# Seven-product projections of six key heads and of the key latents, through memory, ahead of the attention

## The chip, the cores and the metric

The kernel runs on one core of one Trainium2 chip. The metric is the device time of one execution in microseconds. The engines are TensorE (PE; its weight loads are PEld), VectorE (DVE), ScalarE (ACT), GpSimd (POOL) and SyncE (SP); the last issues most of the DMAs, and POOL issues some.

## What is computed

One layer of a streaming encoder with two groups of attention heads that share one input projection, followed by an output projection and a gated feed-forward part. Rows: 512 frames of a new stream with 16 meta tokens ahead, and 64 frames of a running stream with 128 cached rows: T = 592 rows, 2048 wide, all in 32-bit floats.

```python
h = rmsnorm(x, norm_attn_g)
z = h @ w_in          # columns: Q of 8 heads | K of 8 | V of 8 | query latents 512 | key latents 256 | rotary key 64
# group A, 8 differential heads (two 64-wide halves c share one V of 128):
s = einsum('bqhcd,bkhcd->bhcqk', qd, kd) * DIFF_SCALE + bias
p = softmax(where(visible, s, neg));  p = p[:, :, 0] - lam * p[:, :, 1]
o_d = rmsnorm(p @ vd, diff_subln_g) * (1 - lam_init)
# group B, 8 heads over normalised latents with a rotary key:
o_m = latent_attention(...)
x = x + concat(o_d, o_m) @ w_out
x = x + (silu(h2 @ w_gate) * (h2 @ w_up)) @ w_down      # h2 = rmsnorm(x, norm_ffn_g)
```

New keys, values and latents are outputs too.

## The kernel before, in words

Every 32-bit product is made of three fast ones: weights and data are split into a high and a low part (ACT writes the high part at L156, `wh`; DVE subtracts it for the low part at L153, `wl`), and `wh*xh`, `wh*xl`, `wl*xh` are added up in one PSUM bank. A projection of 128 columns (`project`, L225) takes 16 blocks of 128 input rows x 3 products x 2 halves of the tokens, 96 matmuls of 296 columns (288 where only the queries' 576 rows are wanted). Its weights come in two loads of 512 KB (`wr`, two buffers, on SP's queue).

Stages:

1. To 47 us: x is transposed block by block (`transpose_x`), scaled by the norm's gain, split into `xh` and `xl`, which stay on chip; the unscaled block is stored to `xspill` (L484). Beside it head 0's Q and K are projected into `ps0` and `ps1` (`project_both`). The norm's factor of each row is not applied yet: `rb`, a tile with it, scales each projection's result.
2. 47 to about 495 us: the eight differential heads. `diff_attend` (L639) makes the scores in pieces of up to 400 columns (tile `sp`, two banks; L108 on TensorE, with q and its low part), DVE adds the bias and takes the row's extreme (L665), ACT takes the exponential (L669), DVE weights the two halves (L673 to L677, tiles `ls`, `e`, `p`). Products with V follow, then the norm of the result, whose factor DVE works out in three steps of 576 columns (`rsqrt_apart`, L178, L180, L182). While a head is attended, the projections of later heads (`projections`, L725: Q, K and V of each head, in this order) fill TensorE between the pieces. A projection's result is scaled by DVE into a tile `z` (queries L732, keys L739, values L790), turned by `twin_queries`, `keys` and `values` into operands (`q00h` and so on, `kk`, `vh`, `vl`), and transposed for the outputs (tiles `pna`, `pnb`; `natural`, L568). `pck` is the transposed cached key.
3. 495 to 745 us: the latent heads, with the output projection as fill. `second_part` projects query latents (four column blocks), key latents (blocks 4 and 5) and the rotary key.
4. To the end: the rest of the output projection, then the feed-forward part, which already multiplies by seven products (`winograd`, L1262). Its sums of weights (L1300, POOL and DVE) and of tokens (`difference`, L1230 on POOL, split at L1218 on ACT and L1219 on DVE, after ACT's scaling at L1363) are the nearest relatives of the new stage's rows.

What sets the order: for stages 2 and 3 the class `Streams` (L39) advances the generators; each names the time until it goes on (`yield 3.0`), or a list of generators that it waits for (`yield [att[h - 2]]`: until head h - 2's attention is done), or takes a PSUM bank (`take("ps")`), and among the ready ones the lowest rank goes. `projections` has rank 25, below all attention work. TensorE's instructions keep the order in which they are issued; the other engines' are ordered by a scheduler. Each engine runs its own list in order, so a row that waits holds up all behind it. `skew` (L339) copies a bias row into a skewed form in memory on POOL's queue; `diff_attend` loads it on SP's queue (tile `bias`) and clears a corner of it with a memset on POOL (L642).

Of the kernel before, what the change touches and what calls it, by code (L numbers as in the profile page):

```python
# [19 lines left out]
P = 128  # L20
# [78 lines left out]
class OrderedTensorEngine:  # L99
# [5 lines left out]
    def matmul(self, out, lhsT, rhs, start, stop):  # L105
        n = int(np.prod(rhs.shape[1:]))
        self.streams.now += max(n, 256) * (0.00042 if rhs.dtype == F32R else 0.00168)
        self.tc.keep_in_program_order(self.pe.matmul(out, lhsT, rhs, start=start, stop=stop))  # L108
# [7 lines left out]
def encoder_step(  # L116
# [213 lines left out]
    xspill = dp.tile([KC, P, TQ], F32, name="xspill")  # L330
# [15 lines left out]
    with ExitStack() as ph:  # L346
# [42 lines left out]
        with tc.tile_pool(name="xn", bufs=1, reuse_waits="tile") as xn:  # L389
# [83 lines left out]
            def transpose_x(kc):  # L473
# [11 lines left out]
                store(xspill[kc], xt[:, 0:TQ])  # L485
# [64 lines left out]
        pss.close()  # L550
        pst = ph.enter_context(tc.tile_pool(name="pst", bufs=1, space=PSUM, reuse_waits="tile"))
        pso = ph.enter_context(tc.tile_pool(name="pso", bufs=1, space=PSUM, reuse_waits="tile"))
        psv = pss.enter_context(tc.tile_pool(name="psv", bufs=1, space=PSUM, reuse_waits="tile"))
# [171 lines left out]
        def projections():  # L725
# [3 lines left out]

            def queries(h, ps):  # L730
                z = ztile()
                V.scalar_tensor_tensor(hv(z, TQ), ev(ps, QH), DH ** -0.5, hv(rb, TQ),  # L732
                                       op0=ALU.mult, op1=ALU.mult)
                st.give("ps", 2.0)
                twinned[h] = st.spawn(0, twin_queries(qs[h % 2], z))

            def new_keys(h, ps):
                z = ztile()
                V.tensor_tensor(hv(z), ev(ps), hv(rb), op=ALU.mult)  # L739
                st.give("ps", 2.0)  # L740
# [3 lines left out]
            def row_factors():  # L744
                yield 4.0
                for name in ("tp", "po"):
                    yield from st.take(name)
                main, own = tbank("rm"), obank("ro")
                for j, (o, n) in enumerate(tok):
                    PE.matmul(main[:, o:o + n] if o < SEQ else own[:, 0:n], rc[0:n, j:j + 1].to_broadcast([n, P]),  # L750
                              ident[0:n, 0:n], start=True, stop=True)
                V.tensor_copy(rb[:, 0:SEQ], main)
                V.tensor_copy(rb[:, SEQ:T], own[:, 0:OWN])
                for name in ("tp", "po"):
                    st.give(name, 2.0)

            def first_rows():
                yield from row_factors()
                queries(0, ps0)
                yield 3.0  # L760
# [1014 lines left out]
```

## Time and profile before

| | us |
|---|---|
| median of 3 runs | 2362.17 (2360.29 to 2363.19) |
| profiled execution | 2363.54 |
| its span, first to last instruction | 2361.8 |
| TensorE busy in the span | 2331.1 (99%) |
| VectorE busy | 1862.5 (79%) |
| ScalarE busy | 1131.1 (48%) |
| GpSimd busy | 676.8 (29%) |

How to read it: the page gives busy times and shares over the span. A group's row names the line, the engine, the operation, output <- inputs, the shape, how many there were, and after the bar the busy time and the mean of one in ns, then the idle time ahead of them and what ended it. A timeline row begins with the start and the duration in us; in brackets stands the idle time ahead of it and what ended that. A row marked x2 stands for two instructions. A row of the windows begins with the stretch and its length, and then gives the busy time of PE, PEld, DVE, ACT and POOL with the number of instructions, the granted TensorE clock as a share of full speed, the DMA's share and GB/s. A row of the DMA issues gives the KB of one and the median us from issue to landing. Line numbers are those of the kernel before unless the text says otherwise.

### The profile page before, as it was taken

What the parts mean: (1) busy time and instruction counts of PE and PEld (TensorE: products, weight loads), DVE (VectorE), ACT (ScalarE), POOL (GpSimd) and SP (SyncE); (2) the same over time, 40 slices, a digit from 0 to 9 for tenths busy, and PEclk for the clock granted to TensorE, in tenths of its full rate; (3) what the DMA queues carried; (4) which work ended last, traced back from release to release, by engine and by line L of the source; (5) the groups of instructions that cost most, each with busy time, mean ns of one, the idle gap of its engine ahead of it and who ended that gap; (6) DMA issues with size and microseconds to landing.
All of it is one profiled execution on the core that took longest, in us unless ns stands there. A gap on an engine that the chain in (4) does not pass through costs nothing. (4 is left out here: it accounts for less than half of the span.)

```text
span 2361.8 us, 43545 instructions
## 1 busy us (share of the span) xinstructions
PE 2331.1 (99%) x17336; PEld 2299.9 (97%) x17336; DVE 1862.5 (79%) x2777; ACT 1131.1 (48%) x2005; POOL 676.8 (29%) x419
## 2 busy tenths in 40 slices
PE   9999999999999999999999999999999999999998
PEld 8999999999999999999999999999999999999997
DVE  6667776676666789888898888888888888888884
ACT  6455555444454554444454454454454333333435
POOL 0000000120001446555555555554555111111110
PEclk9999999999999999999999999999999999999999
DMA  8433343263334643444444544544546884654532
GB/s 257 118 93 93 102 118 86 73 188 96 114 93 156 186 151 102 158 154 136 158 149 136 163 142 138 168 133 147 167 132 201 312 289 137 230 181 156 181 90 99
DMA packets 361626, 353.10 MB, mean 150 GB/s; under 512 B 23751, under 2 KB 318446, under 8 KB 361422
## 3 DMA queue, kind: packets, MB, share of 16 engines
q1 hardware_dynamic: 359150, 345.78, 46.4%
q0 software_dynamic: 992, 3.48, 0.5%
q8 instruction: 136, 2.23, 0.4%
q10 hardware_dynamic: 1280, 1.06, 0.2%
q14 instruction: 68, 0.56, 0.1%
HBM read 268.82 MB, written 82.34 MB: 149 GB/s over the span
## 5 line engine op out<-in xcount | busy, mean ns | idle before, releaser
L1315 PE MATMUL m<-b,wh 128*128 128x288 f32 x7280 | 1062.9, 295 | 7.8 <-ACT wh L156 3.3
L1315 PEld LDWEIGHTS m<-b,wh 128*128 128x128 f32 x7280 | 994.6, 188 | 13.0 <-ACT wh L156 9.2
L1319 PE MATMUL m<-b,wl 128*128 128x288 f32 x3640 | 581.1, 296 | 2.3 <-DVE wl L153 2.0
L1319 PEld LDWEIGHTS m<-b,wl 128*128 128x128 f32 x3640 | 515.7, 189 | 4.7 <-DVE wl L153 4.5
L153 DVE TENSOR_TENSOR wl<-raw,wh 128x1024 fp32r<-128x1024 f32 (+2 forms) x347 | 477.3, 1377 | 38.9 <-ACT wh L156 38.4
L156 ACT ACTIVATE wh<-raw 128x1024 fp32r<-128x1024 f32 (+2 forms) x347 | 313.6, 904 | 363.7 <-PE m L1315 320.2
L1300 POOL TENSOR_TENSOR ws<-raw 128x1024 f32<-128x1024 f32 (+2 forms) x85 | 173.0, 2036 | 662.4 <-DVE wl L153 339.8
L156 ACT ACTIVATE wh<-ws 128x512 fp32r<-128x512 f32 (+2 forms) x248 | 196.7, 793 | 286.5 <-PE m L1315 126.0
L153 DVE TENSOR_TENSOR wl<-ws,wh 128x512 fp32r<-128x512 f32 (+2 forms) x248 | 240.3, 969 | 7.7 <-PE m L1319 4.3
L108 PE MATMUL ps<-xh,wh 128*128 128x296 f32 (+1 forms) x992 | 222.8, 306 | 0.3 <-ACT xh L160 0.3
L108 PE MATMUL ps<-xl,wh 128*128 128x296 f32 (+1 forms) x992 | 215.2, 298 | 0.4 <-DVE xl L161 0.3
L108 PE MATMUL ps<-xh,wl 128*128 128x296 f32 (+1 forms) x960 | 207.8, 298 | 0.0
L1574 DVE TENSOR_TENSOR y<-y,m 128x288 f32<-128x288 f32 x280 | 126.2, 451 | 65.3 <-PE m L1319 64.2
L1466 DVE TENSOR_TENSOR c<-c,s 128x288 fp32r<-128x288 f32 x172 | 170.3, 990 | 0.0
L108 PEld LDWEIGHTS ps<-xh,wh 128*128 128x128 f32 x992 | 159.9, 190 | 3.3 <-issue 1.1
L108 PEld LDWEIGHTS ps<-xl,wh 128*128 128x128 f32 x992 | 160.6, 189 | 1.1 <-DVE xl L161 0.9
L108 PEld LDWEIGHTS ps<-xh,wl 128*128 128x128 f32 x960 | 155.5, 189 | 0.0
L153 DVE TENSOR_TENSOR wl<-wr,wh 128x1024 fp32r<-128x1024 f32 (+1 forms) x109 | 117.3, 1077 | 42.6 <-ACT wh L156 38.9
L1300 POOL TENSOR_TENSOR raw<-raw 128x1024 f32<-128x1024 f32 (+1 forms) x46 | 141.0, 3064 | 3.5
L156 ACT ACTIVATE wh<-wr 128x1024 fp32r<-128x1024 f32 (+1 forms) x111 | 102.0, 918 | 81.4 <-PE ps L108 57.8
L1412 DVE TENSOR_TENSOR c<-c,m 128x288 f32<-128x288 f32 x171 | 73.1, 447 | 79.1 <-PE m L1319 41.1
L1485 POOL TENSOR_TENSOR c<-c,rb 128x576 f32<-128x576 f32 x44 | 74.9, 1702 | 138.0 <-ACT c L1484 138.0
(400 smaller groups left out, 3031.9 us busy)
## 6 DMA issues: line engine op xcount, KB each, us to landing
raw<-in_ffn_w_gate SPq DMA_DIRECT2D x44, 1024.0 KB, 6.1
raw<-in_ffn_w_up SPq DMA_DIRECT2D x44, 1024.0 KB, 7.9
b<-opspill SPq DMA_DIRECT2D x147, 288.0 KB, 6.0
raw<-in_ffn_w_down SPq DMA_DIRECT2D x32, 1024.0 KB, 5.9
wr<-in_w_in SPq DMA_DIRECT2D x57, 512.0 KB, 4.1
opspill<-s SPq DMA_DIRECT2D x43, 576.0 KB, 3.1
opspill<-c SPq DMA_DIRECT2D x43, 576.0 KB, 6.7
raw<-in_ffn_w_down SPq DMA_DIRECT2D x8, 1280.0 KB, 6.1
```

The lines of the kernel that those rows point to most:

```text
L108: self.tc.keep_in_program_order(self.pe.matmul(out, lhsT, rhs, start=start, stop=stop))
L153: V.tensor_tensor(lo, src, f32(hi), op=ALU.subtract)
L156: S.activation(hi, src, AF.Copy)
L1300: (G if p == 5 or p == 7 and within else V).tensor_tensor(x, y, z, op=ALU.add if p == 5 else ALU.subtract)
L1315: PE.matmul(banks[p], wh[:, k, :], x, start=first and new and k == 0 and x is hi, stop=False, skip_group_check=not new)
L1319: PE.matmul(banks[p], wl[:, k, :], hi, start=False, stop=last and k == n - 1, skip_group_check=not new)
L1412: V.tensor_tensor(c, c, banks[p], op=ALU.add)
L1466: V.tensor_tensor(src[:, k].bitcast(F32R), src[:, k], f32(hi[:, k]), op=ALU.subtract))
L1485: G.tensor_tensor(g[:, f, :], g[:, f, :], rb2, op=ALU.mult)
L1574: V.tensor_tensor(c, c, banks[p], op=ALU.add)
```

## The change

`xspill` keeps all 592 rows of x, and a new tile in memory, `zspill`, holds eleven projection results. Between stage 1 and the attention stands a new stage:

- V0 is projected first; within it `rb` is made and the results of Q0 (kept on chip as `z_first`) and K0 (to `zspill`) are scaled. Then Q1. Both results go to `zspill` (V0: 7, Q1: 8).
- Beside them the generator `token_sums` builds operands: for each of eight pairs of row blocks it loads the two blocks back from `xspill`, ACT scales them by the gain, POOL makes four differences of token halves in a chain (t = b12 - b11, t = b22 - t, t7 = b22 - b12, t = b21 - t; t is overwritten), and each is split into a high and a low part that stay on chip (32 tiles `s4` to `s7`).
- `seven` is called four times: key heads 1 and 2, 3 and 4, 5 and 6, and the two key latents. A call takes two blocks of 128 columns as the halves of a 2x2 block product (row blocks in even and odd positions, tokens in two halves): four weight loads of 512 KB (`quarter`; two into new tiles `wa`, two into the two buffers `wr`), four sums of weights (one on POOL, three on DVE), and seven products of 24 matmuls of 296 columns in the order 1, 2, 5, 6, 3, 7, 4, added up in PSUM or by DVE and ACT. The two results are scaled by `rb` and stored to `zspill`.

The attention then takes K0 to K6, V0, Q1 and the latents 4 and 5 from `zspill` by DMAs on POOL's queue (`spilled_rows`, L859 of the changed kernel), and `projections` makes only Q of heads 2 to 7, K of head 7 and V of heads 1 to 7.

```diff
-    xspill = dp.tile([KC, P, TQ], F32, name="xspill")
+    xspill = dp.tile([KC, P, T], F32, name="xspill")
+    zspill = dp.tile([11, P, T], F32, name="zspill")
...
+            def token_sums():
+                for m in range(KC // 2):
+                    rows_ = [sa.tile([P, T], F32, name="xr", tag=f"xr{t}", bufs=2) for t in range(2)]
+                    for t, r in enumerate(rows_):
+                        load(r, xspill[2 * m + t])
+                        S.activation(r, r, AF.Copy, scale=gA[:, 2 * m + t:2 * m + t + 1])
+                    (b11, b12), (b21, b22) = (halves(r) for r in rows_)
+                    yield
+                    def operand7(p, src):
+                        hl = sa.tile([P, 2, TH], F32R, name=f"s{p}_{m}")
+                        split(hl[:, 0], hl[:, 1], src)
+                        operands7[m, p] = hl[:, 0], hl[:, 1]
+                    t = sa.tile([P, TH], F32, name="ts", tag="ts", bufs=2)
+                    t7 = sa.tile([P, TH], F32, name="t7", tag="t7")
+                    G.tensor_tensor(t, b12, b11, op=ALU.subtract)
+                    operand7(5, t)
+                    G.tensor_tensor(t, b22, t, op=ALU.subtract)
+                    operand7(6, t)
+                    yield
+                    G.tensor_tensor(t7, b22, b12, op=ALU.subtract)
+                    operand7(7, t7)
+                    G.tensor_tensor(t, b21, t, op=ALU.subtract)
+                    operand7(4, t)
+                    yield
...
+            for n, _ in enumerate(project(pv0, w_in[:, OFF_V:OFF_V + P], xs1, ready=(both[4], both[5]))):
+                if n == 3:
+                    spread_factors()
+                    z_first = scaled_rows(ps0, None, QUERY_SCALE)
+                    scaled_rows(ps1, 0)
+                if n % 2:
+                    next(building)
+            scaled_rows(pv0, 7)
+            pq1 = pjt()
+            for n, _ in enumerate(project(pq1, w_in[:, P:2 * P], xs1, n=QH)):
+                if n % 2:
+                    next(building)
+            scaled_rows(pq1, 8, QUERY_SCALE)
...
+                w = sa.tile([P, KC // 2, P], F32, name="wsum")
+                steps = {5: (G, w, a21, a22, ALU.add), 6: (V, w, w, a11, ALU.subtract),
+                         3: (V, a12, a12, w, ALU.subtract), 7: (V, a21, a11, a21, ALU.subtract)}
...
+                for p, name in ((1, "a"), (2, "c"), (5, "b"), (6, "a"), (3, "b"), (7, "a"), (4, "d")):
...
+                    split(wh, wl, src[p])
+                    for k in range(KC // 2):
+                        for i in range(2):
+                            PE.matmul(banks[name], wh[:, k, :], operands7[k, p][i],
+                                      start=new and k + i == 0, stop=False, skip_group_check=not new)
+                    for k in range(KC // 2):
+                        PE.matmul(banks[name], wl[:, k, :], operands7[k, p][0],
+                                  start=False, stop=k == KC // 2 - 1, skip_group_check=not new)
...
+            for h in (1, 3, 5):
+                seven([OFF_K + (h + i) * P for i in range(2)], (h, h + 1))
+            seven((OFF_CKV, OFF_CKV + P), (9, 10))
...
+            def spilled_rows(i, n=T):
+                z = ztile()
+                G.dma_start(z[:, 0:n], zspill[i, :, 0:n])
+                return z
...
             for h in range(H):
+                ps = None
+                if h > 1:
+                    ps = yield from taken()
+                    yield from project(ps, w_in[:, h * P:(h + 1) * P], xs1, n=QH)
+                    yield [scored[h - 2]]
+                queries(h, ps)
+                ps = None
+                if h == H - 1:
+                    ps = yield from taken()
+                    yield from project(ps, w_in[:, OFF_K + h * P:OFF_K + (h + 1) * P], xs1)
+                if h:
+                    yield [nat[2 * h - 1], nat[2 * h - 2]]
+                new_keys(h, ps)
                 if h:
                     ps = yield from taken()
+                    yield from project(ps, w_in[:, OFF_V + h * P:OFF_V + (h + 1) * P], xs1)
                     if h >= 2:
+                        yield [att[h - 2]]
```

Three places of the order. First ACT, from the row factors on. Before (`wh_816` is the second weight split of V0, the `q00h` and `kk` rows make head 0's operands):

```order
L156 ACTIVATE wh_816<-wr_814 128x1024
L156 ACTIVATE vh_811<-cv_826 128x128
L620 ACTIVATE q00h_658<-z_731 64x576 x2
L611 ACTIVATE kk0_769<-z_767 64x576
L611 ACTIVATE kk1_770<-z_767 64x576
```

The changed kernel, late in the building (`xr` are rows loaded back, `s5_6` is the operand of product 5 for pair 6, `wh_1115` the high part of product 2's weights):

```order
L568 ACTIVATE xr_994<-xr_994,gA_189 128x592
L156 ACTIVATE s4_4_978<-ts_951 128x296
L568 ACTIVATE xr_1020<-xr_1020,gA_189 128x592
L156 ACTIVATE s6_5_1009<-ts_1002 128x296
L156 ACTIVATE s7_5_1013<-t7_1003 128x296
L156 ACTIVATE s5_6_1029<-ts_1026 128x296
L156 ACTIVATE wh_1115<-wa_1075 128x1024
```

The splits of token sums now stand among the weight splits, and product 2's weights stand behind pair 6's first sum.

Second TensorE, in head 2's scores. Before (`sp<-kk` are score pieces, `ps<-xh` and `ps<-xl` rows of a projection):

```order
L108 MATMUL sp<-kk_1710,q00h 128x272
L108 MATMUL sp<-kk_1710,q00l 128x272
L108 MATMUL ps<-xh_88,wh 128x296 x2
L108 MATMUL ps<-xl_104,wh 128x296 x2
L108 MATMUL ps<-xh_88,wl 128x296 x2
L108 MATMUL sp<-kk_1711,q01h 128x272
L108 MATMUL sp<-kk_1711,q01l 128x272
L108 MATMUL ps<-xh_89,wh 128x296 x2
L108 MATMUL ps<-xl_105,wh 128x296 x2
L108 MATMUL ps<-xh_89,wl 128x296 x2
```

The same place in the changed kernel:

```order
L112 MATMUL pck<-ident,ck 128x128
L108 MATMUL sp<-kk_2511,q00h 128x272
L108 MATMUL sp<-kk_2511,q00l 128x272
L108 MATMUL sp<-kk_2512,q01h 128x272
L108 MATMUL sp<-kk_2512,q01l 128x272
L108 MATMUL sp<-kk_2511,q00h 128x400
L108 MATMUL sp<-kk_2511,q00l 128x400
L108 MATMUL sp<-kk_2512,q01h 128x400
L108 MATMUL sp<-kk_2512,q01l 128x400
L108 MATMUL sp<-kk_2511,q00h 128x264
```

The rows of a projection that stood between the pieces are gone there; they come again three pieces later.

Third POOL, where the attention begins. Before (`p5`, `pm`, `vm` are padded operands, `tsk` the skewed bias in memory):

```order
L339 DMA tsk_72<-trow_71 128x656
L564 MEMSET pm_670 80x512
L564 MEMSET vm0_671 80x128
L564 MEMSET vm1_672 80x128
L566 MEMSET p5_676 128x256
L642 MEMSET bias_1006 64x64
L339 DMA tsk_72<-trow_71 128x656
```

The changed kernel (`z_2022` is K0's rows, `z_2026` V0's, `z_2030` Q1's):

```order
L655 TENSOR_TENSOR wsum_1764<-wa_1760,wa_1758 128x1024
L859 DMA z_2022<-zspill_67 128x592
L691 MEMSET pm_2013 80x512
L691 MEMSET vm0_2014 80x128
L691 MEMSET vm1_2015 80x128
L693 MEMSET p5_2019 128x256
L920 DMA zl4_5360<-zspill_67 128x592
L769 MEMSET bias_2103 64x64
L340 DMA tsk_73<-trow_72 128x656
L859 DMA z_2026<-zspill_67 128x592
L859 DMA z_2030<-zspill_67 128x576
```

The loads of K0's, V0's and Q1's rows stand in POOL's list, the last two behind the bias memset.

More of the change, by code (lines that the diff above doesn't have):

```diff
@@ L103, in __init__, with matmul @@
         self.tc, self.streams, self.pe = tc, streams, tc.nc.tensor
-    def matmul(self, out, lhsT, rhs, start, stop):
+    def matmul(self, out, lhsT, rhs, start, stop, **kw):
         n = int(np.prod(rhs.shape[1:]))
         self.streams.now += max(n, 256) * (0.00042 if rhs.dtype == F32R else 0.00168)
-        self.tc.keep_in_program_order(self.pe.matmul(out, lhsT, rhs, start=start, stop=stop))
+        self.tc.keep_in_program_order(self.pe.matmul(out, lhsT, rhs, start=start, stop=stop, **kw))
     def transpose(self, out, in_, identity):
@@ L484, in transpose_x @@
                 V.tensor_copy(xt, sp)
-                store(xspill[kc], xt[:, 0:TQ])
+                store(xspill[kc], xt)
                 if rider:
@@ L551, in encoder_step @@
         pst = ph.enter_context(tc.tile_pool(name="pst", bufs=1, space=PSUM, reuse_waits="tile"))
         pso = ph.enter_context(tc.tile_pool(name="pso", bufs=1, space=PSUM, reuse_waits="tile"))
-        psv = pss.enter_context(tc.tile_pool(name="psv", bufs=1, space=PSUM, reuse_waits="tile"))
+        second["bank"] = pss.enter_context(tc.tile_pool(name="psb", bufs=2, space=PSUM, reuse_waits="tile"))
         zl = ph.enter_context(tc.tile_pool(name="zl", bufs=1, reuse_waits="tile"))
@@ L742, in new_keys @@
                 nat[2 * h] = st.spawn(0, keys(h, z, kk[h % 2]))
[L744 to L760, printed above, removed]
-                new_keys(0, ps1)
-                headed["done"] = True
-            headed = dict(done=False)
             kk = [None, None]
             twinned = [None] * H
-            st.spawn(0, first_rows())
             for h in range(H):
+                ps = None
[3 more added lines that the diff above has]
+                    yield [scored[h - 2]]
@@ L772, in projections @@
                     if h >= 2:
-                        yield [scored[h - 2]]
-                    queries(h, ps)
-                    ps = yield from taken()
-                    yield from project(ps, w_in[:, OFF_K + h * P:OFF_K + (h + 1) * P], xs1)
-                    yield [nat[2 * h - 1], nat[2 * h - 2]]
-                    new_keys(h, ps)
-                    ps = yield from taken()
-                else:
-                    ps = psv.tile([P, 2, 512], F32, name="ps")
-                yield from project(ps, w_in[:, OFF_V + h * P:OFF_V + (h + 1) * P], xs1, ready=None if h else (both[4], both[5]))
@@ L805, in projections @@
                     st.spawn(2, key_latents())
+                if i in (4, 5):
+                    zs[i] = zl.tile([P, T], F32, name=f"zl{i}", tag=f"zl{i}")
+                    G.dma_start(zs[i], zspill[5 + i])
+                    continue
                 off = OFF_CQ + i * P
```

98 lines of the change are left out of this document (80 added, 18 removed).

## The prediction

> **What bounds it now.** I read the page's busy times first, then the windows of busy time in the attention stage, then TensorE's waits there, and last the timelines around the two places where the new stage begins and ends.
>
> ```profile
> PE 2331.1 (99%) x17336; PEld 2299.9 (97%) x17336; DVE 1862.5 (79%) x2777; ACT 1131.1 (48%) x2005; POOL 676.8 (29%) x419
> 60.00:120.00 60.00, 60.00 (x455) 59.80 (x454) 37.34 (x86) 27.99 (x60) 0.91 (x3) 1.00 0.43 115
> 300.00:360.00 60.00, 60.00 (x452) 59.23 (x451) 41.54 (x99) 32.29 (x69) 2.82 (x5) 1.00 0.39 111
> PE pn L112 <- ACT nn L937: 1.6, 2, 1.1
> ```
>
> TensorE is busy 60.00 of 60.00 us in both windows (columns after the stretch: PE, PEld, DVE, ACT, POOL, clock, DMA share, GB/s), at clock 1.00, and its longest sum of waits between 60 and 540 us is 1.6 us. So a matmul taken out is a gain at its full price, and any wait given to TensorE is a loss at its full price. DVE, 37 to 42 us of 60, is covered by projections that stand between the score matmuls as fill.
>
> **A. Fewer matmuls.** A pair of 128 column blocks takes 192 matmuls of 296 columns now (16 row blocks, two halves, three split products, twice) and 7 products x 24 = 168 then; four pairs save 96.
>
> ```profile
> 47.21 0.43 PE L108 MATMUL ps<-xh,wh 128*128 128x296 f32 x2
> ...
> 52.95 1.05 PE L108 MATMUL rm<-ident,rc 128*128 128x128 f32 x8
> ```
>
> Between these two starts, 5.74 us, stand 21 rows of 2, 42 matmuls: 0.137 us each. 96 x 0.137 = 13.2 us gained. All of it is on the path. The feed-forward part is left as it is.
>
> **B. Building the operands.** V0 (13.1 us, with 1.0 us for the row factors), Q1 (12.7 us) and products 1 and 2 (24 x 0.137 = 3.3 us each) cover the building: from 47.2 us TensorE would reach product 5, the first with a token sum, at 80.6 us. The rows for the building:
>
> ```profile
> 46.82 3.04 SPq L137 DMA_DIRECT2D wr<-in_w_in  x2
> wr<-in_w_in SPq DMA_DIRECT2D x57, 512.0 KB, 4.1
> xo<-xspill SPq DMA_DIRECT2D x16, 256.0 KB, 3.6
> 54.81 1.06 ACT L156 ACTIVATE wh<-wr 128x1024 fp32r<-128x1024 f32 x1 [6.52 <-PE ps L108]
> 773.04 0.78 ACT L1363 ACTIVATE xg<-x,gT 128x576 f32<-128x576 f32 x1 [2.44 <-DVE x L1361]
> L1230 POOL TENSOR_TENSOR bs<-xg x16: 792/808/1017, 755.4 to 853.9; 128x288 f32<-128x288 f32 x16
> L1230 POOL TENSOR_TENSOR bs<-xg,bs x16: 800/882/1190, 761.1 to 858.9; 128x288 f32<-128x288 f32 x16
> L1218 ACT ACTIVATE b<-bs x32: 424/430/447, 756.5 to 860.1; 128x288 fp32r<-128x288 f32 x32
> L1219 DVE TENSOR_TENSOR b<-bs,b x32: 445/447/1275, 756.9 to 861.5; 128x288 fp32r<-128x288 f32 x32
> L1300 POOL TENSOR_TENSOR ws<-raw 128x1024 f32<-128x1024 f32 x43 | 113.6, 2643 | 254.4 <-DVE wl L153 246.4 <-DVE c L1424 8.0
> ```
>
> ACT's first scaling stands behind a weight split that waits for TensorE until 54.8 us and ends at 55.9 us; with one 0.78 us scaling POOL's first difference starts near 56.6 us. The last operand needed by product 5 ends the 31st difference: 31 x 0.845 us (mean of 808 and 882) + one weight sum of 2.64 = 28.8 us, so 85.4 us, and with ACT's high part of that operand (0.43) and of the weight sum (1.06) product 5 starts at 86.9 us at best, 6 us late. But a difference is written over the tile that the split before it still reads, so about one round trip of high part and low part (0.43 + 0.45, with the handover about 1.0) per pair of row blocks is exposed: eight of them give 95 us. Bounds 6 and 20 (two round trips exposed in some pairs); I take the single round trip: **+14**. In ACT's order product 2's weight split already stands behind an operand of the seventh pair, so the first stall shows at product 2, and shifts part of the wait there, not more. DVE's two-input rows are slower beside a running POOL row (b<-xg, mean 1643 against 447 ns), and lie inside this.
>
> ```profile
> L1219 DVE TENSOR_TENSOR b<-xg,b x24: 446/1643/1686, 755.2 to 857.4; 128x288 fp32r<-128x288 f32 x24
> ```
>
> **C. Between the sevens.** The tiles of the lower weights are the two used for streaming weights, so the next pair's loads start only when product 4's low part has been made. Then come a load of 4.1 us, the second right behind it (about 1 us more, an estimate), the weight sum, 2.64, and its high part, 1.06: with handovers about 10 us until product 5 can start. Against them stand products 1 and 2, 6.6 us, and about 2 us left of product 4. About 1.3 us shows at each of three boundaries: **+4**, from 0 (covered) to 6.
>
> **D. From the last seven to the attention.** TensorE's next rows are the transposes of V0's and K0's rows, which come back from memory, through POOL's queue. There V0's load stands behind the bias memset, which waits for a bias load.
>
> ```profile
> 107.68 0.14 POOL L642 MEMSET bias<- 64x64 f32 x1 [50.74 <-DMA bias<-tsk]
> 108.12 0.52 POOL L339 DMA_DIRECT2D tsk<-trow  x1 [0.29 <-issue]
> bias<-tsk SPq DMA_DIRECT2D x8, 264.0 KB, 3.8
> cos<-c_cos POOLq DMA_DIRECT2D x1, 296.0 KB, 3.1
> 55.98 1.38 ACT L620 ACTIVATE q00h<-z 64x576 fp32r<-64x576 f32 x2
> ```
>
> The bias load goes out about 0.6 us after the stage's tiles are free and lands 3.8 us later; memset and skew take 0.14 + 0.29 + 0.52; a load of this size from POOL's queue took 3.1 us: 8.5 us before the first transpose. Then one bank serves five transposes in a chain, each followed by a copy of about 0.7 us, one behind ACT's q00h (1.38 us); queries' fill stands behind all of them. Near 15.8 us in all, of which TensorE works 1.5: **+14**, from 10 (copies overlap) to 18 (the load takes as long again).
>
> **E. The attention.** Each head keeps two projections of 13 us as fill instead of three, while its DVE work stays. In the order, the generator of projections waits for an older head's attention with V done, and seven score pieces of head 2 stand in one row without fill (heads 3 to 5 alike; head 1 has twelve). During the seven, DVE must do this:
>
> ```profile
> 184.67 0.78 DVE L739 TENSOR_TENSOR z<-ps,rb 128x592 f32<-128x592 f32 x1 [0.23 <-PE ps L108]
> ...
> 187.77 1.23 DVE L153 TENSOR_TENSOR wl<-wr,wh 128x1024 fp32r<-128x1024 f32 x1
> 188.91 0.75 DVE L178 TENSOR_TENSOR sq<-sq,r 128x576 f32<-128x576 f32 x1
> 189.58 0.43 DVE L665 CUSTOM_DVE_ANT_0 e<-sp,bias 128x272 f32<-128x272 f32 x1
> ...
> 191.61 0.36 DVE L675 TENSOR_SCALAR e<-e,ls 128x272 f32<-128x272 f32 x1
> 192.01 0.50 DVE L677 SCALAR_TENSOR_TENSOR p<-e,ls 128x272 f32<-128x272 f32 x1
> ...
> 192.73 0.76 DVE L180 SCALAR_TENSOR_TENSOR sq<-sq,r 128x576 f32<-128x576 f32 x1
> 193.40 0.57 DVE L665 CUSTOM_DVE_ANT_0 e<-sp,bias 128x400 f32<-128x400 f32 x1
> ...
> 194.39 0.76 DVE L182 SCALAR_TENSOR_TENSOR r<-sq,r 128x576 f32<-128x576 f32 x1
> ...
> 196.93 0.43 DVE L665 CUSTOM_DVE_ANT_0 e<-sp,bias 128x264 f32<-128x264 f32 x1
> ```
>
> z 0.78, two of 272 (0.86), two small key rows (about 0.35), two of 400 (1.14), L178, L180 and L182 (2.27), the weights' low part (1.23), L675 and L677 (0.86), one of 264 (0.43) and two small rows of sums (0.33): 8.3 us to the seventh piece, and about 0.9 us until fill follows; TensorE's own work there (14 score rows and a transpose, about 0.13 us each) is about 1.9. So 7 us of idle in each of heads 2 to 5, 10 in head 1, 3 in head 6: **+41**. The low end, 27, takes the normalization (L178, L180, L182, 2.3 us) and one handover out of each stretch; the high end, 57, adds a stretch like these in heads 6 and 7, which lose latent projections as fill. The later key rows cost nothing more: a load of 3.1 us is asked for a head ahead.
>
> **F. The clock.**
>
> ```profile
> 6.00:8.00 2.00, 0.68 (x3) 0.30 (x3) 0.00 (x0) 0.24 (x1) 0.00 (x0) 1.00 1.07 313
> ...
> 10.00:14.00 4.00, 4.00 (x19) 3.98 (x20) 2.63 (x4) 1.10 (x2) 0.00 (x0) 0.57 1.12 287
> 14.00:16.00 2.00, 2.00 (x18) 2.00 (x18) 1.52 (x2) 1.02 (x4) 0.00 (x0) 1.00 1.15 233
> ```
>
> At the start TensorE stood idle for much of 6 to 8 us at clock 1.00, was granted 0.57 from 10 to 14 us though busy, and 1.00 again from 14 us: 4.00 x 0.43 = 1.7 us lost behind one such gap. The three long gaps (B, D, head 1) give **+5**, from 0 to 14 (eight gaps).
> The Trainium skill, "TensorE: Matmul & The Clock Gate", section "Part 1: The HAM clock gate", says that an idle window of about 3.4 us halves the clock and that about 3.4 us of work restores it; the rows at 6 to 16 us agree, and by that rule every gap of B to E costs extra, which speaks against the change.
>
> **Sum.** -13.2 + 14 + 4 + 14 + 41 + 5 = +64.8. The profiled execution took 2363.54 us (span 2361.8), so 2428.3; the runs' median, 2362.17, is 1.4 lower: **2427 us**. Lows: -13.2 + 6 + 0 + 10 + 27 + 0 = +29.8, 2392; highs: -13.2 + 20 + 6 + 18 + 57 + 14 = +101.8, 2464.
>
> **Rivals.**
> *Every gap is clocked down.* Five more gaps (heads 2 to 6) lose 1.7 us each, +9: 2436. For it: 7 us is longer than the gap at 6 to 8 us. Against: the seven pieces run in between, so no gap is whole. Chance 0.27.
> *The attention keeps pace.* DVE has 18 us of 60 free at 300 to 360 us; were its work ahead of the pieces done early, E would fall away and two long gaps remain in F (+4): -13.2 + 14 + 4 + 14 + 4 = +22.8, 2385. Against:
>
> ```profile
> 347.84 0.14 POOL L642 MEMSET bias<- 64x64 f32 x1 [43.04 <-DMA bias<-tsk]
> ```
>
> From the memset at 107.68 to this one are five heads, 48.0 us each. Without one projection a head has 48.0 - 13.1 = 35 us of matmuls, and DVE 41.54 / 60 x 48.0 = 33 us of work: no slack for a fixed order. Chance 0.11.
> *Faster: everything is covered.* If POOL starts by 50 us and its round trips hide, product 5 is ready by 81 us, B is 0; were the spilled rows loaded while the last seven runs, D is 6; with C, E and F at 0 the sum is -7: 2355. It decides if B to F stay under 13 us together. For it: POOL is idle (0.91 us of 60) and SP's queue is light. Against: V0's load stands behind a memset, and B's six us come from POOL rows alone. Chance 0.05.
> That the change doesn't do what it says is excluded: the order has 24 matmuls for each of the seven products.
>
> **Range and chances.** The forecast has 0.54, the clock 0.27, the attention in pace 0.11, faster 0.05; 0.03 remain for an end between the last two, within 0.2% (4.7 us, about what a measurement of this kernel can tell from no change). So slower 0.92, same 0.03, faster 0.05. The range runs from the attention in pace, 2385, to 2458, short of all highs together; the two ends of the chances left out are 0.08 below and about 0.1 above.
>
> **What would show it.** TensorE's waits should be: up to 14 us around products 2 and 5 of the first pair, released by ACT's splits behind POOL; about 1.3 us at each later pair; about 14 us after the last product 4, released by a spilled-row load on POOL's queue; some 7 us per head at sp, released by DVE. The clock should fall below 1.00 after the first and third. It would be wrong if the score pieces wait under 2 us per head (then 2385), or if POOL's differences end by 81 us.

## The result and the profile after

The changed kernel took 2468.22 us (median of 4 runs, 2465.07 to 2468.82), the kernel before 2361.70 in the same session: 1.0448 times as long, with a 95% interval of 1.0430 to 1.0466. It is slower by 106 us; the forecast was slower by 65, and 2468 lies above the range.

The page of the profile after, busy times:

```profile
PE 2356.6 (96%) x17240; PEld 2313.5 (94%) x17240; DVE 1914.2 (78%) x2849; ACT 1173.3 (48%) x2081; POOL 721.7 (29%) x466
```

TensorE has 96 matmuls fewer, as counted, and yet is busy 25.5 us longer. The span grew from 2361.8 to 2466.8 us, so its idle time grew by 79.5 us; and since 13.2 us of work went, about 38.7 us of its busy time are work at a lower clock. Both can be seen in the windows. Four stretches of the profile after (columns behind the stretch: its length, then busy time of PE, PEld, DVE, ACT, POOL, the granted clock, DMA share, GB/s):

```profile
74.00:106.00 32.00, 16.14 (x85) 15.43 (x84) 26.76 (x29) 18.82 (x35) 20.96 (x20) 0.73 0.38 109
180.00:200.00 20.00, 7.97 (x55) 7.36 (x53) 10.81 (x15) 7.80 (x14) 4.44 (x11) 0.72 0.82 249
220.00:480.00 260.00, 229.49 (x1551) 218.37 (x1551) 178.29 (x441) 138.69 (x308) 9.69 (x24) 0.90 0.33 91
580.00:612.00 32.00, 18.85 (x84) 15.44 (x85) 23.77 (x35) 14.20 (x31) 5.48 (x5) 0.63 0.59 168
```

These are the first pair of the new stage, the seam to the attention, the attention, and the entry to the latent heads. TensorE's waits over the span name what it waited for (us in total, times, longest):

```profile
PE sp L108 <- DVE nm L792: 23.6, 19, 4.2
PE m L108 <- ACT wh L156: 15.9, 3, 12.5
PE pna L112 <- DMA z<-zspill: 11.3, 1, 11.3
PE ps L108 <- ACT mxh L1007: 6.4, 1, 6.4
...
PE pn L112 <- DVE kr L1017: 3.8, 1, 3.8
...
PE ps L108 <- DVE mxl L1008: 2.8, 1, 2.8
```

The first three are the attention, the building and the seam. The last three are new and belong to the entry of the latent heads, of which the sum of the prediction had nothing.

Cut into windows of 1 us, each place gives its idle time (length less busy time) and its lost clock (busy time x (1 - granted clock)), summed:

| place in the profile after | forecast | idle | lost clock |
|---|---|---|---|
| A, 96 matmuls | -13.2 | -13.2 | |
| B, building, 40 to 110 us | +14 | 15.9 | 4.5 |
| C, between the sevens, 110 to 187 | +4 | 0.1 | 0.0 |
| D, seam, 187 to 220 | +14 | 15.5 | 3.4 |
| E, attention, 220 to 580 | +41 | 34.9 | 18.8 |
| entry to the latent heads, 580 to 612 | 0 | 13.2 (3.3 before) | 7.0 |
| F, clock | +5 | | 33.7 |

With the column's -13.2, idle time 76.3 and lost clock 33.7 this makes 96.8 of the 105.0 us between the two spans. Of the rest, 1.7 us are clock lost in the first 40 us and some 4 us idle time in the second half of the feed-forward part, from 1900 us on, where nothing was changed. The first differs between the executions of all the kernels here (0.0 to 3.4 us); the remaining 2.5 us aren't assigned.

What a stretch without fill looks like, TensorE in head 5 of the profile after:

```profile
442.52 0.45 PE L108 MATMUL sp<-kk,q10h 128*128 128x400 f32 x1 [0.61 <-DVE nm L792]
...
443.84 0.39 PE L108 MATMUL sp<-kk,q10h 128*128 128x264 f32 x1 [0.32 <-DVE nm L792]
...
448.54 0.59 PE L108 MATMUL sp<-kk,q10h 128*128 128x264 f32 x1 [4.19 <-DVE nm L792]
```

The wait is where the order said, 4.19 us, for DVE. Behind it the same piece of 264 columns takes 0.59 us in place of 0.39: the clock is down.

### The profile page after: what moved, and what is told of

It is laid out like the page before. It is cut to its first block, busy times and chain, and to the rows that moved or that the text cites. A ratio compares the mean times of both kernels' runs of the same rounds, so it can differ in the third digit from the quotient of the medians.

```text
span 2466.8 us, 43688 instructions
## 1 busy us (share of the span) xinstructions
PE 2356.6 (96%) x17240; PEld 2313.5 (94%) x17240; DVE 1914.2 (78%) x2849; ACT 1173.3 (48%) x2081; POOL 721.7 (29%) x466
## 5 line engine op out<-in xcount | busy, mean ns | idle before, releaser
L1690 DVE TENSOR_TENSOR y<-y,m 128x288 f32<-128x288 f32 x280 | 126.0, 450 | 66.8 <-PE m L1435 64.8
L108 PE MATMUL ps<-xh,wh 128*128 128x288 f32 (+1 forms) x736 | 169.6, 313 | 0.1
L108 PE MATMUL ps<-xl,wh 128*128 128x288 f32 (+1 forms) x736 | 163.6, 304 | 0.0
L108 PE MATMUL ps<-xh,wl 128*128 128x288 f32 (+1 forms) x704 | 155.7, 303 | 0.0
L108 PEld LDWEIGHTS ps<-xh,wh 128*128 128x128 f32 x736 | 123.1, 197 | 2.9 <-issue 1.1
L108 PEld LDWEIGHTS ps<-xl,wh 128*128 128x128 f32 x736 | 123.2, 195 | 0.6 <-DVE xl L161 0.4
L156 ACT ACTIVATE wh<-wr 128x1024 fp32r<-128x1024 f32 (+1 forms) x95 | 84.9, 894 | 74.8 <-PE ps L108 50.0
L153 DVE TENSOR_TENSOR wl<-wr,wh 128x1024 fp32r<-128x1024 f32 (+1 forms) x93 | 96.3, 1035 | 28.4 <-ACT wh L156 25.0
L108 PEld LDWEIGHTS ps<-xh,wl 128*128 128x128 f32 x704 | 117.7, 195 | 0.0
```

Of the source, the lines that this page charges most:

```text
L153: V.tensor_tensor(lo, src, f32(hi), op=ALU.subtract)
L156: S.activation(hi, src, AF.Copy)
L1690: V.tensor_tensor(c, c, banks[p], op=ALU.add)
```

## The experiments

All edits are made to the changed kernel (2468.2 us). The theory: the new stage and the fill that was moved away leave waits at four places, and each place costs its idle time and then, on top, the clock that the idle time takes down. The rivals differ from run to run.

**The latents back as fill.**

```diff
-            seven((OFF_CKV, OFF_CKV + P), (9, 10))
...
-                if i in (4, 5):
-                    zs[i] = zl.tile([P, T], F32, name=f"zl{i}", tag=f"zl{i}")
-                    G.dma_start(zs[i], zspill[5 + i])
-                    continue
```

> The changed kernel with the fourth call of the seven products taken out; the two key latents are projected as fill ahead of the latent heads again. The changed kernel took 2468.2 us. Theory (each place without fill costs its idle time and, on top, the half clock): the waits on mxh, mxl and kr at the entry of the latent heads (13.2 us idle and 7.0 us of lost clock between 580 and 612 us, against about 3 us idle before) go; 24 matmuls, 3.3 us, come back: about 2454 us. Rival (the entry waits for splits that come late anyway, whatever fill there is): only the 3.3 us come back, about 2471 us.

Measured: 2449.57 us (1.0369, interval 1.0351 to 1.0388), 18.6 us less than the changed kernel, though 3.3 us of matmuls came back. The place where the entry now lies:

```profile
560.00:600.00 40.00, 36.44 (x260) 34.44 (x259) 33.99 (x46) 21.76 (x39) 9.53 (x10) 1.00 0.60 175
```

Clock 1.00 and 3.6 us of idle, as before the change (3.3); the waits on mxh, mxl and kr are gone. So the two latent projections were the cover of the splits for the output projection (`mix_operand`): taken out, they cost 18.6 + 3.3 = 22 us. Of this, 9.6 us of idle time and 7.0 of lost clock stand at the entry, 3.7 of idle time in heads 6 and 7 (480 to 580 us: 4.4 in the changed kernel, 0.7 here), and 1.6 are clock lost in the first 40 us, which the edit doesn't touch.

**The keys back as fill.**

```diff
-            for h in (1, 3, 5):
-                seven([OFF_K + (h + i) * P for i in range(2)], (h, h + 1))
...
-                if h == H - 1:
+                if h:
                     ps = yield from taken()
```

> The changed kernel with K of heads 1 to 6 projected as fill in the attention again; the stage still makes the operands, and by seven products the key latents alone. Theory: the attention's 35 us of idle and 18.8 us of lost clock go, 72 matmuls (9.9 us) come back: about 2468.2 - 54 + 10 = 2424 us, and TensorE's waits at the score pieces are gone. Rival (the attention is slow for the reading back of rows through POOL's queue and for its changed order, not for missing fill): V0, K0 and Q1 still come from memory, so no more than half of it goes, about 2450 us.

Measured: 2417.18 us (1.0227, 1.0212 to 1.0242), 51 us less. The attention:

```profile
300.00:360.00 60.00, 60.00 (x449) 59.18 (x449) 44.92 (x111) 32.02 (x71) 1.91 (x5) 1.00 0.38 109
```

TensorE is full again at clock 1.00, with the spilled rows of V0, K0 and Q1 still read back through POOL. The rival falls. The gain is 7 us above the 44 that were expected, most of it at the seam, which now stands behind one call of `seven` and idles 10.0 us in place of 15.5. What is left over the kernel before, 54 us, is building, seam and entry.

**One pair alone.**

```diff
-            for h in (1, 3, 5):
-                seven([OFF_K + (h + i) * P for i in range(2)], (h, h + 1))
-            seven((OFF_CKV, OFF_CKV + P), (9, 10))
+            seven([OFF_K + (1 + i) * P for i in range(2)], (1, 2))
...
-                if h == H - 1:
+                if h > 2:
...
-                if i in (4, 5):
...
```

> The changed kernel with seven products for key heads 1 and 2 alone; K of heads 3 to 7 and the latents are fill again. Theory (each key head taken out of the fill costs 11.5 us in the stage, half of 168 matmuls, and gives the attention back far less; by the run with the keys back 51 us for six, 8.5 us each): from 2449.6 us with three pairs it falls by 4 x 8.5 = 34 us, to about 2416 us. Rival (the loss sits in the first heads, as head 1's long stretch lets one think, and the later pairs gain their 3.3 us): it stays above 2440 us.

Measured: 2421.80 us (1.0245, 1.0230 to 1.0260), 27.8 us less than with three pairs and the latents as fill: 7.0 us for each key head given back, somewhat less than the 8.5 expected, and far from the rival's 2440. So the loss isn't all in the first heads. But head 1's stretch is still there with keys 1 and 2 alone moved: 8.3 us of lost clock between 150 and 220 us of this run.

**Fill held back.** Nothing is added; of each V projection the last row blocks wait for the pieces that had no fill.

```diff
+                if b == 1:
+                    begun[h]["done"] = True
...
-                    yield from project(ps, w_in[:, OFF_V + h * P:OFF_V + (h + 1) * P], xs1)
+                    for n, _ in enumerate(project(ps, w_in[:, OFF_V + h * P:OFF_V + (h + 1) * P], xs1)):
+                        if h >= 2 and n == 5:
+                            yield [begun[h - 1]]
+                        yield 0
```

> The changed kernel with one thing held back: of each V projection of heads 2 to 7 the last ten row blocks wait until the head before has begun its second block of scores, so they stand between the seven pieces that had no fill. Nothing is added or taken out. Theory (idle and lost clock come from the order, since fill is used up ahead of the pieces): 4 x 5.3 + 6.3 us of idle and 18.8 us of lost clock go, about 2468.2 - 45 = 2423 us, somewhat more if the products with V now lack fill. Rival (DVE bounds the attention, 33 us of work a head against 35 us of matmuls, so idle time only moves): the waits turn up at the products with V, the time stays above 2455 us.

Measured: 2480.41 us (1.0493, 1.0477 to 1.0509): 12 us slower than the changed kernel, where the theory said 45 faster. TensorE's waits between 220 and 480 us:

```profile
PE tp L112 <- DVE kk L739: 7.0, 5, 1.4
PE pna L112 <- DVE pk2l L153: 5.0, 4, 1.3
PE pnb L112 <- ACT na L725: 3.4, 5, 0.7
PE po L108 <- ACT o L301: 3.4, 5, 0.7
PE sp L108 <- DVE nm L794: 1.9, 5, 0.4
```

The wait at the score pieces (sp) fell from 23.6 us in the whole span to 1.9 here, and, as the rival had it, the same time came back at the transposes and products with V: 26.7 us of idle and 23.0 of lost clock in this window, against 30.5 and 18.8. So this other order of the same fill gains nothing, and the run with the keys back shows that more fill does: there is too little of it. The theory's word "order" falls; that no order at all would do better is not shown.

**Fewer matmuls still.** Of each Q projection of heads 2 to 7 only 12 of 96 matmuls are left.

```diff
+                if few and kc not in (0, KC - 1):
+                    yield 0
+                    continue
                 mm3([ps[:, 0, 0:n], ps[:, 1, 0:n]], wh[:, k, :], wl[:, k, :],
...
-                    yield from project(ps, w_in[:, h * P:(h + 1) * P], xs1, n=QH)
+                    yield from project(ps, w_in[:, h * P:(h + 1) * P], xs1, n=QH, few=True)
```

> The changed kernel with 12 of the 96 matmuls of each Q projection of heads 2 to 7; the other 84 are left out, so the queries are incomplete, and weights are loaded and split as before. 6 x 84 x 0.133 = 67 us of TensorE work are gone from the attention. Theory (a head's length is set by the chain of DVE, ACT and single PSUM banks, of some 40 us, once fill no longer covers it): the time falls by far less than 67 us, by 0 to 25, and the idle time grows by 45 or more. Rival (TensorE's own work still sets the length): it falls by 50 us or more, below 2418 us.

Measured: 2484.24 us (1.0512, 1.0494 to 1.0529), 16 us slower with 67 us of TensorE's work left out, where a gain of up to 25 was expected. The attention:

```profile
220.00:480.00 260.00, 192.96 (x1011) 165.68 (x1010) 173.81 (x434) 133.27 (x301) 12.27 (x24) 0.74 0.32 89
```

In 260 us TensorE has 540 rows fewer than the changed kernel, idles 67.0 us in place of 30.5 and loses 49.3 us of clock in place of 18.8. A head takes (469.50 - 322.88) / 3 = 48.9 us by its bias memsets, against (455.95 - 326.95) / 3 = 43.0 in the changed kernel and 48.0 in the kernel before. The rows, this run's first, then the changed kernel's:

```profile
322.88 0.14 POOL L772 MEMSET bias<- 64x64 f32 x1 [27.03 <-DVE e L805]
469.50 0.14 POOL L772 MEMSET bias<- 64x64 f32 x1 [40.23 <-DVE e L805]
...
326.95 0.14 POOL L769 MEMSET bias<- 64x64 f32 x1 [41.01 <-DVE nm L792]
455.95 0.14 POOL L769 MEMSET bias<- 64x64 f32 x1 [38.44 <-DMA bias<-tsk]
```

So a head's length is not TensorE's amount of work any more. TensorE's few steps (transposes, score pieces, products with V) stand in a chain with DVE and ACT. Why the head became longer stays open: the lost clock grew by 30.5 us in the window, but 18.1 us of the idle time are a wait that this edit made, of projections for the low part of their weights (`wl`).

**Unread matmuls where TensorE waits, in the seams.**

```diff
                     split(wh, wl, src[p])
+                    for _ in range({2: 88, 5: 16}.get(p, 0) if spilled[0] == 1 else 0):
+                        PE.matmul(banks[name], xh[0][:, 0:P], xh[1][:, 0:TH], start=True, stop=True)
...
             pa = tbank("pna")
+            for _ in range(warm.pop() if warm else 0):
+                PE.matmul(pa[:, 0:TH], xh[0][:, 0:P], xh[1][:, 0:TH], start=True, stop=True)
```

> The changed kernel with matmuls on data at hand, whose results nobody reads, put where TensorE waits in the first pair (88 ahead of product 2, 16 ahead of product 5) and ahead of the first transposes of the attention (80): 184 x 0.137 = 25 us of work in 26 us of idle time. Theory (the half clock follows idle time): the clock stays at 1.00 up to the first transposes and the 4.5 + 3.4 us of lost clock go, most of it, about 2462 us. Rival (the clock falls for another reason, as the load of the other engines): the clock in these places stays low and the 25 us turn into a delay of about as much as the clock is down, 2468 us or more.

Measured: 2474.32 us (1.0466, 1.0450 to 1.0482), 6 us slower. Its clock in the building:

```profile
94.00:96.00 2.00, 1.83 (x14) 1.59 (x12) 1.60 (x3) 1.77 (x4) 1.53 (x3) 1.00 0.00 0
96.00:98.00 2.00, 0.00 (x0) 0.00 (x0) 1.61 (x3) 1.07 (x3) 1.60 (x3) 1.00 0.00 0
98.00:100.00 2.00, 1.17 (x5) 1.17 (x6) 2.00 (x3) 1.12 (x2) 0.56 (x1) 0.54 0.00 0
100.00:102.00 2.00, 2.00 (x10) 2.00 (x10) 1.97 (x4) 0.33 (x1) 0.00 (x0) 0.50 0.00 0
102.00:104.00 2.00, 2.00 (x10) 2.00 (x10) 2.00 (x3) 1.49 (x2) 0.00 (x0) 0.50 0.56 159
104.00:106.00 2.00, 2.00 (x13) 2.00 (x13) 1.09 (x2) 0.71 (x2) 0.00 (x0) 0.75 0.34 103
106.00:108.00 2.00, 2.00 (x17) 2.00 (x16) 0.45 (x1) 0.69 (x1) 0.00 (x0) 1.00 0.14 30
```

While the unread matmuls run the clock is 1.00 (in the changed kernel it was 0.50 at 92 to 94 us). They end too early for product 5: one gap of 3.0 us is left, and it takes the clock to 0.50 for some six us. At the seam, DVE's order changed with the added rows and a copy came 5.3 us late. So the run shows when the clock falls, but its time can't be read as the price of the clock.

**The same in the first pair alone, long enough.** 100 and 40 in place of 88 and 16, and none at the seam.

> The changed kernel with unread matmuls in the first pair alone, now enough for both gaps: 100 ahead of product 2 (13.7 us for a gap of 12.5) and 40 ahead of product 5 (5.5 us for 2.6). Theory (the clock falls only where TensorE has stood idle for some 3 us): the clock stays at 1.00 from 60 to 187 us, the 4.5 us of lost clock go, and up to 2 us are lost to unread matmuls that outlast the gap: about 2465 us. Rival (the clock falls in the building for the load of the other engines): it falls below 1.00 between 80 and 110 us though TensorE is busy, and the time is 2468 us or more.

Measured: 2468.08 us (1.0446, 1.0427 to 1.0464).

```profile
74.00:106.00 32.00, 30.99 (x229) 30.52 (x228) 27.32 (x31) 19.66 (x36) 22.11 (x21) 1.00 0.37 106
```

The clock stays at 1.00 and the lost 4.5 us are 0.0, with DVE, ACT and POOL as busy as before: the rival falls. The time stayed, since the unread work was 19.0 us for a loss of idle time from 15.9 to 1.5: it outlasted the gaps by 4.6 us, which took the gain.

**Unread matmuls between the pieces.** 30 of them in heads 2 to 5, at the wait of 4.2 us.

```diff
+                        if 2 <= h <= 5 and (b, c, i) == (3, 0, 0):
+                            spare = pjt()
+                            for _ in range(30):
+                                tc.keep_in_program_order(nc.tensor.matmul(
+                                    spare[:, 0, 0:TH], xh[0][:, 0:P], xh[1][:, 0:TH], start=True, stop=True))
```

> The changed kernel with 30 unread matmuls (4.1 us) in each of heads 2 to 5, exactly where TensorE waits 4.2 us for DVE between two score pieces. Theory (the clock follows TensorE's idle time): in these four stretches the clock stays at 1.00, the 1.8 + 2.6 + 3.0 + 3.2 = 10.6 us of lost clock go, the score pieces wait as long as before, now behind work: about 2458 us. Rival (DVE's chain sets the length of a head and TensorE's clock beside it costs nothing): the clock goes up and the time stays at 2468 us within 3.

Measured: 2458.41 us (1.0400, 1.0384 to 1.0415), 9.8 us less than the changed kernel, by 120 matmuls that nobody reads. Head 5 of this run:

```profile
440.55 4.17 PE L799 MATMUL ps<-xh,xh 128*128 128x296 f32 x30
444.89 0.39 PE L108 MATMUL sp<-kk,q10h 128*128 128x264 f32 x1 [0.18 <-DVE nm L792]
```

The piece behind the wait takes 0.39 us again, not 0.59. Lost clock between 220 and 480 us is 9.4 us in place of 18.8, and what is left is head 1's. From this piece in head 2 (at 318.13 us in the changed kernel, 319.25 here) to the end of TensorE's wait for `mxh` (584.38 and 578.46) it took 266.3 us in the changed kernel and 259.2 here: 7.0 us of the 10.6 came back there. The rest of the 9.8 lies outside this stretch, where nothing was changed. So the lost clock goes when the idle time is filled, and the larger part of it is on the path; the rival (TensorE's clock costs nothing beside DVE's chain) falls.

**Unread matmuls as fill.** The same through the planner: 40 unread matmuls a head (80 for head 1) in the projections' free bank, from the second block of scores on.

```diff
+                        yield [begun[h - 1]]
+                        busy_bank = yield from taken()
+                        for _ in range(20 if h == 2 else 10):
+                            for i in range(4):
+                                PE.matmul(busy_bank[:, 0, 0:TH], xh[0][:, 0:P], xh[1][:, 0:TH], start=True, stop=True)
+                            yield 0
+                        st.give("ps", 0.0)
                         yield [att[h - 2]]
```

> The changed kernel with 40 unread matmuls (80 for head 1; 5.5 us and 11 us) as added fill for each head from the second block of scores of the head before on, in the free bank of the projections. Nothing is taken out. Theory (the lost clock hangs on idle TensorE): most of the 18.8 us of lost clock in the attention goes, the idle time is filled with work that nobody needs: about 2453 us, if the unread matmuls fall into the gaps. Rival (the attention's length is set by DVE's and ACT's chain, and TensorE's clock is not on it): the clock goes up and the time stays at 2468 us within 4.

Measured: 2491.60 us (1.0551, 1.0533 to 1.0569), 23 us slower. The waits at the score pieces fall from 23.6 to 6.0 us and idle time between 220 and 480 us from 30.5 to 21.6, but waits at the transposes grow (`tp`, from 3.1 to 9.2) and the lost clock is 17.4 us, hardly less. So lost clock doesn't simply follow the sum of idle time; this run decides nothing about its price.

**The seam alone.** No operands, no seven products; V0 and Q1 ahead, K0, V0 and Q1 through memory.

```diff
-            for h in (1, 3, 5):
-                seven([OFF_K + (h + i) * P for i in range(2)], (h, h + 1))
-            seven((OFF_CKV, OFF_CKV + P), (9, 10))
...
-                if n % 2:
-                    next(building)
...
-                if h == H - 1:
+                if h:
...
```

> The changed kernel without operands and seven products: only V0 and Q1 are projected ahead and go through memory with K0; K of all later heads and the latents are fill again. Against the kernel before no matmul is saved. Theory (the seam to the attention costs by itself 11 to 15 us of idle and 3 us of lost clock): 2362 + 13 to 19, about 2378 us. Rival (the seam is long only behind the seven products, whose last stores and buffers it waits for): the rows lie ready by the time the attention begins, within 5 us of the kernel before.

Measured: 2365.32 us against 2363.11 of the kernel before (1.0010, 1.0000 to 1.0019): no loss that can be told. TensorE idles 1.2 us between 40 and 100 us, clock 1.00. The rival is right: reading these three rows back through POOL's queue costs nothing where they lie ready.

**Rows kept on chip.**

```diff
-                    scaled_rows(ps1, 0)
+                    k_first = scaled_rows(ps1, None)
...
-            scaled_rows(pv0, 7)
+            v_first = scaled_rows(pv0, None)
...
-                c1, c2 = ztile("c"), ztile("c")
+                c1, c2 = ctile(0), ctile(1)
```

> The changed kernel with V0's and K0's rows kept on chip from the stage to the attention (the results of the seven products take the building's row tiles instead, and Q1's rows are scaled after the building). Theory (the seam to the attention is the way of V0's rows through memory): TensorE's wait of 11.3 us for the spilled rows goes and with it the 3.4 us of lost clock, some 4 us for the chain of transposes and copies stay: about 2454 us. Rival (the bias load and the query rows keep the seam as long, or the row tiles now shared stretch the building): 2463 us or more.

Measured: 2462.03 us (1.0424, 1.0407 to 1.0440), 6 us less, not 14. The seam idles 12.2 us in place of 15.5, and its wait has another name:

```profile
PE pnb L112 <- ACT na L728: 8.3, 1, 8.3
```

ACT stood 3.7 us at the cached V rows, loaded on SP behind the last results' store, with that copy in its list behind them. The seam's loads start only as the stage ends; with one taken away, another is nearly as late.

**Two differences on DVE.**

```diff
-                    G.tensor_tensor(t7, b22, b12, op=ALU.subtract)
+                    V.tensor_tensor(t7, b22, b12, op=ALU.subtract)
...
-                    G.tensor_tensor(t, b21, t, op=ALU.subtract)
+                    V.tensor_tensor(t, b21, t, op=ALU.subtract)
```

> The changed kernel with two of the four differences of each pair of row blocks (those for products 7 and 4) made on DVE instead of POOL. Theory (the building is late because 32 differences of 0.8 to 1.0 us with their round trips stand in a row on POOL, 42 us): POOL's chain is shorter by 16 rows, some 15 us, the 15.9 us of idle and 4.5 us of lost clock nearly go: about 2451 us. Rival (ACT's and DVE's splits, not POOL, pace the building): the gap ahead of product 2 stays over 8 us, 2460 us or more.

Measured: 2461.50 us (1.0421, 1.0402 to 1.0440), 7 us less, between the two. The gap ahead of product 2, 12.5 us in the changed kernel, is now

```profile
82.14 0.61 PE L108 MATMUL m<-xh,wh 128*128 128x296 f32 x1 [4.94 <-ACT wh L156]
```

and two smaller ones follow (2.3 and 1.7 us). Idle time in the building is 8.9 us, but lost clock still 4.7: with half of POOL's differences gone, 7.0 of the building's 15.9 us of idle time go. The rest, which these waits put to ACT's and DVE's splits, was not taken apart.

No run points to a version that beats the kernel before: each pair of key or latent projections moved out of the fill costs more than it saves.

## Why the prediction was right or wrong

Between the sum of the prediction, +64.8, and the 105.0 us between the two spans lie 40.2 us. F, the clock, makes 28.7 of them, idle time at the entry of the latent heads 9.9. B and D add 3.4, C and E take 10.0 away, and 8.2 lie outside the table.

*A and the sign: right.* The count of matmuls fell by 96, and the change was slower for the reasons given: the work taken out is cheaper than the cover that goes with it.

*B, the building: right in size, +14 against 15.9 us of idle.* It shows at product 2 first, 12.5 us, and at product 5 with 2.6, as ACT's order had it, though the prediction expected only part of the wait at product 2. A difference on POOL took 1.0 us in the mean, not the 0.845 of the sum (32 in 32.0 us). The two differences on DVE show that POOL's row of differences makes at least 7.0 us of the idle time.

*C: wrong, +4 against 0.1.* The later pairs wait for nothing. As forecast, the last load goes out when product 4's low part is made, at 113.07 us, and the high part of the weight sum is ready 8.2 us later, at 121.26 (forecast: 10). The step that failed is the cover, "products 1 and 2, 6.6 us, and about 2 us left of product 4": the low part was made before product 4 began at 114.44, so all of product 4 was left, and product 5 starts at 124.31, 11.2 us after the load.

*D, the seam: size right, +14 against 15.5; mechanism half wrong.* The prediction put V0's load behind the bias memset. It was, but the memset was done when POOL still waited (POOL's queue, profile after):

```profile
190.93 0.14 POOL L769 MEMSET bias<- 64x64 f32 x1 [1.28 <-DMA bias<-tsk]
...
194.30 0.54 POOL L859 DMA_DIRECT2D z<-zspill  x1 [2.39 <-DMA zspill<-c]
```

The load went out 2.4 us later, when the last results' store had landed. In the program, the results of `seven` and the rows read back share the buffers of `ztile`, so a buffer comes free with the store. And the seam without operands and seven products costs nothing: it is long only behind them.

*E, the attention: right, +41 against 34.9 us of idle.* The seven pieces without fill were found in the order, and 5.3 us of idle came of it in each of heads 2 to 5 where 7 were forecast. Head 1 idles 6.3 where 10 were forecast, but only 2.2 of them at its score pieces; its longest wait is at a transpose:

```profile
258.70 0.52 PE L112 MATMUL tp<-ident,p 128*128 128x128 f32 x3 [3.06 <-DVE kk L739]
...
273.24 0.59 PE L108 MATMUL sp<-kk,q10h 128*128 128x264 f32 x1 [1.91 <-DVE nm L792]
```

And the reason given was the order, while holding fill back, which took the waits from the pieces, gained nothing.

*The entry of the latent heads: missing, 16.9 us.* The prediction took the latents' 26 us of matmuls as moved, and looked for their cover only in heads 6 and 7, for the high end. What they covered were the splits ahead of the output projection. The step "name the work that is covered by what is moved" was not done for this fill. Of the 16.9 us, 9.9 are idle time and 7.0 lost clock, which also stand in F's 33.7.

*F, the clock: the main error, +5 against 33.7 us.* The step that failed is "4.00 x 0.43 = 1.7 us lost behind one such gap", times three gaps. The rival "every gap is clocked down", chance 0.27, had the places in the heads right, not the entry, but the same price, 1.7, and gave 14 us in all. The rows show 1.8 to 3.4 us at the seam and in heads 2 to 5, 4.5 in the building, 7.0 at the entry and 8.2 in head 1. The price was read from one place, where work without a break followed the gap. And the rows there show no long gap. Between 6 and 10 us TensorE idled 2.0 of 4.0 us, 1.33 at the longest (profile before, a row of the timeline and one of the windows):

```profile
8.01 0.26 PE L112 MATMUL pxt<-ident,xo 80*128 80x80 f32 x1 [1.33 <-DMA xo<-in_meta_tokens]
...
8.00:10.00 2.00, 1.32 (x9) 0.90 (x9) 1.57 (x3) 1.70 (x3) 0.00 (x0) 1.00 1.10 336
```

So these rows agree with about 3.4 us for the way back (1.7 us lost at half clock), but not, as the prediction has it, with an idle window of about 3.4 us ahead of it. They speak against its argument that short gaps with pieces in between count less. In a stretch where short waits go on, the clock stays down for all of it: the window below is head 1's, of the profile after, with TensorE busy 78% of 20 us at clock 0.51.

```profile
260.00:280.00 20.00, 15.63 (x54) 12.53 (x55) 13.91 (x49) 9.27 (x26) 0.00 (x0) 0.51 0.09 26
```

*The rival "the attention keeps pace"* falls: it needed E at 0. Its counter-argument, 35 us of matmuls against 33 of DVE work, was right in direction, but neither sum sets the head's length. With 13.1 us of matmuls taken out, a head fell from 48.0 to 43.0 us; with another 11 out it took 48.9.

The account for one key head, by the three heads from 326.95 us on: the stage pays 168 / 2 x 0.137 = 11.5 us for it, and the attention gives back 48.0 - 43.0 = 5.0. That is a loss of 6.5 us each, and 7.0 were measured between one and three pairs, 8.5 between none and three, where the shorter seam is in it.

## What to carry to other kernels

Work that fills waits is worth less than its own time: when it is moved out, only the part that the waits beneath it don't use comes back, so add up for each stretch what the moved work covers before counting the gain. On TensorE an exposed wait is paid again through the clock, and the price of that is read from a stretch of the same kind, with its short waits, not from one place with unbroken work behind it. A test with unread matmuls in the gap, no longer than the gap, tells the two apart.

## What the runs showed of the hardware

A gap needn't be long to take the clock down. In the run with fill held back, TensorE stood in waits of at most 1.3 us each from 339 to 342 us, busy 1.18 of 3.00 us, and was granted about half for the next ten us:

```profile
339.00:342.00 3.00, 1.18 (x8) 0.63 (x6) 1.69 (x3) 1.01 (x2) 0.00 (x0) 1.00 0.00 0
342.00:352.00 10.00, 7.23 (x27) 6.02 (x28) 3.04 (x13) 4.25 (x14) 0.00 (x0) 0.52 0.16 45
```

And the way back can take longer than the gap: in the run with unread matmuls in the seams, one gap of 3.0 us was followed by work without a break from 98.8 us, and the clock was back at 1.00 only at about 105, which cost 3.1 us. In the changed kernel, a gap of 2.6 us ended at 99.75, and the clock was at 0.50 from about 100 and back 3.5 us after the restart.

The Trainium skill, "TensorE: Matmul & The Clock Gate", section "HAM oscillation — how this bites in real kernels", has the rule that gaps over about 3.4 us are to be avoided. Here gaps of 3.0 and 2.6 us and a row of waits of at most 1.3 us took the clock down too.

Left open: which link of the chain of TensorE, DVE and ACT sets a head's 43 us; no single one was taken out.
